# Tables of gates and overflow built from 16-bit one-hots that the routing keeps, and the first expert's weights split by other engines in another order

## The chip, the cores and the metric

The program runs on one core of a Trainium2 chip, as one launch. The metric is the device time of one execution in microseconds, the median over several runs. The core has a matrix engine (TensorE, PE in the profile; its weight loads are the track PEld), a vector engine (VectorE, DVE), an activation engine (ScalarE, ACT), GpSimd (POOL) and a queue engine (SyncE, SP) that issues the loads of the weights. Every engine works through its own list of instructions in order; semaphores order them against each other.

## The reference

Two layers. The first mixes tokens by a gated MLP and a gated convolution, the second by sliding-window attention; each is followed by a norm, a mixture of 32 experts (two for each token) and another norm. The change touches the mixture of experts only:

```
g_idx = argmax(x @ w_grp); e_sel = (x @ w_exp)[group g_idx]
top_p, top_i = top_k(softmax(e_sel), 2);  gates = g_p * top_p / sum(top_p)
# rows sorted by expert, in blocks of 128 rows: row_tok, row_gate, blk_e
def run_block(xb, e): return (silu(xb @ wg[e]) * (xb @ wu[e])) @ wd[e]
out = segment_sum(ys * row_gate, row_tok)
```

There are 1024 tokens with 1024 channels; an expert has 512 hidden channels, all in 32-bit floats.

## The kernel before

**Weights.** All weights come in chunks of 1 MB (tiles `raw` and `ry`, 128x2048). For the products each is split in two: ScalarE writes the high part (`h`, line 164), and VectorE subtracts it from the chunk for the low part (`l`, line 165). A 32-bit product is then three TensorE products, h by xh, l by xh and h by xl (lines 204 to 206, `mm3`). `split_until(i)` writes both parts of all chunks up to the i-th; `pump` then issues the next load into the room that came free. An expert has six chunks: two of `w_gate`, two of `w_up`, two of `w_down`. The h and l tiles of chunks lie in two places of two buffers each, so four chunks can be split at a time.

**Routing** (`proj_route`). For each of eight blocks n of 128 tokens: output projection (`pm`), residual and norm (`norm`, on `xr`, with a power on GpSimd at line 258 between the two halves), transposes (`transp`), the router's products (`logits`, into `pl`), the choice of the first and the second expert (`choose`, `choose2`, line 470 and around), a product that counts earlier tokens with the same expert (`rank`), the slot of each token (`place`, which makes a one-hot row `oh` for it), and the table of tokens by expert and slot (`tabulate`, into `pidx`). The steps of the blocks overlap. After the last block's projection the tail is left: `norm`, `transp`, `logits`, `choose`, `choose2`, `rank`, `place` and `tabulate` of block 7, with those of block 6 between them, and the first three chunks of the first expert, whose low parts GpSimd makes there (`eng=nc.gpsimd`). `warm(n)` are products for nothing, on TensorE, between the steps. The tail ends with `idx` (line 598), the table of tokens.

**Experts** (`experts`). `gather(e)` fetches an expert's rows by an indirect transfer that GpSimd issues (line 703). `xpose` transposes them into `pt`, `xsplit` splits them into `xh` and `xl`, `gu` makes the products with gate and up weights (`pg`, `pu`), `hid_pose` transposes and splits the hidden rows, `down` makes the last products and `y_out` adds the rows, times their gates (`sgate`), to the result. The order is written out by hand. Between the products `extra(e)` takes the next piece of a generator: the gates, then the table of gates by slot (`slot_gates`, 16 products into `pgate`, from one-hots `goh` and rows `ga` that GpSimd makes), then the bookkeeping of rows beyond an expert's 128 (`overflow`, 16 products into `pov`, from `ooh` and `orr` that VectorE makes). There are three such places in an expert, each behind `split_until`.

The first expert's split rows lie in the room of the results:

```
th, tl = ("xh", "xl") if e > 0 else ("yt0", "yt1")
h = w.tile([P, 8, P], F32R, name=f"xh{e}", tag=th, bufs=1)
lo = w.tile([P, 8, P], F32R, name=f"xl{e}", tag=tl, bufs=1)
```

A tag with `bufs=1` has one room: a new tile in it waits until all that reads the tile before it is done.

Of the kernel before, what the change touches and what calls it, by code (L numbers as in the profile page):

```python
# [19 lines left out]
P = 128  # L20
# [5 lines left out]
NG = 4  # L26
# [9 lines left out]
def moe_net_kernel(ctx, tc, a, dbg=None):  # L36
# [76 lines left out]
    st = {"load": 0, "split": 0, "hlb": None, "rawb": None, "xT": None,  # L113
# [3 lines left out]
    def pump(eng=nc.sync):  # L117
        while st["load"] < min(len(chunks), st["limit"]):
# [13 lines left out]
            if i == 1:  # L132
                # the first two chunks come in alternate quarters, that the work may start
# [12 lines left out]
    # 32 KB in two halves: the mixers' output, chunks, the norm's rows, heads of q  # L146
# [19 lines left out]

    def split_until(i, eng=None, high=None):
        while st["split"] <= min(i, len(chunks) - 1):
            j = st["split"]
            st["split"] += 1  # L170
            where = chunks[j][1]
            if where in ("a", "b"):
                p = hla if where == "a" else st["hlb"]
                h = p.tile([P, 2048], F32R, name=f"h{j}", tag="h" + where, bufs=2)
                l = p.tile([P, 2048], F32R, name=f"l{j}", tag="l" + where, bufs=2)
            else:
                k = 2 * where[1]
                h = st["xT"][0][:, k:k + 2, :].rearrange("p k f -> p (k f)")
                l = st["xT"][1][:, k:k + 2, :].rearrange("p k f -> p (k f)")
            hs[j], ls[j] = h, l  # L180
# [7 lines left out]
            elif j in (mark["qkv"] - 1, len(chunks) - 1):  # L188
                for o in (0, 1024):
                    split_to(*(c[:, o:o + 1024] for c in (h, l, x)), eng)  # L190
            else:
                split_to(h, l, x, eng, high)
# [3 lines left out]
    def warm(n, ps, tag, bufs):  # L196
        # products for nothing where the tensor engine waits, that its clock stays up
# [12 lines left out]
    # -------------------------------------------------------------- constants  # L210
# [54 lines left out]
    # ------------------------------------------------- bias rows of attention  # L265
# [3 lines left out]
    def bias_rows(w, ps):  # L269
# [11 lines left out]
        # row q lies q further right, so that a plain rectangle of it holds the relative positions  # L281
# [25 lines left out]
            # v, tokens on partitions  # L307
# [26 lines left out]
            # u, channels on partitions  # L334
# [15 lines left out]
            # spatial mixing of v and y_a  # L350
# [12 lines left out]
            # gated convolution  # L363
# [261 lines left out]
    def slot_gates(w, ps, R):  # L625
        pt = ps.tile([P, 512], F32, name="pgate", tag="misc", bufs=1)
        made, used = [], 0
        for make, use in ((4, 0), (2, 0), (4, 4), (6, 6), (0, 0), (0, 6)):
# [10 lines left out]
            if used < 16:  # L639
                yield  # L640
# [810 lines left out]
```

## Time and profile before

| what | value |
|---|---|
| time, median of 3 runs | 2085.58 us (2083.27 to 2086.29) |
| profiled execution, its time from first to last instruction (span) | 2086.2 us |
| TensorE busy | 1931.8 us, 93% |
| VectorE busy | 1580.8 us, 76% |
| ScalarE busy | 1206.1 us, 58% |
| GpSimd busy | 476.9 us, 23% |
| mean rate of the transfers | 253 GB/s |
| mean granted clock of TensorE | 0.962 of full |

The profiled execution has no other time listed than its span; it lies within 0.03% of the median. Busy times are shares of the whole program, whose stages differ; the stages are read apart by their place in time. The routing's tail lies at 340 to 372 us in the first layer and at 1367 to 1399 us in the second, the experts behind each.

### The profile page before, as it was taken

The page shows a single profiled execution, that of the slowest core. Times are in us where ns is not written, and L with a number is a line of the kernel's source. Part 1 is how long each engine was busy: PE and PEld are TensorE (multiplying, and loading weights), DVE is VectorE, ACT ScalarE, POOL GpSimd, SP SyncE. Part 2 cuts the span into 40 slices and gives each one's busy share as a digit, 9 for nine tenths or more (in the row PEclk, how much of TensorE's full clock was granted, in tenths as well). Part 3 has the DMA queues.
Part 4 walks back from the last instruction along what each step waited for, and adds up shares of the span by engine and source line. Part 5 has one row for each costly group of instructions (what it writes and reads, how often), then busy time and mean ns, then how long its engine had stood idle before and what let it go on. Part 6 is the DMA issues. An engine that isn't in the chain of part 4 may idle for free. (4 is left out here: it accounts for less than half of the span.)

```text
span 2086.2 us, 24852 instructions
## 1 busy us (share of the span) xinstructions
PE 1931.8 (93%) x9264; PEld 1565.7 (75%) x9264; DVE 1580.8 (76%) x2020; ACT 1206.1 (58%) x1246; POOL 476.9 (23%) x319
## 2 busy tenths in 40 slices
PE   8999998899999999998598989979999999999990
PEld 7888786687778888887487767757877888888870
DVE  3533587599888888887643996976898888888876
ACT  4211211477677777776454872125777777777763
POOL 0100003622111211212300552146121112112116
PEclk9999998899999999999799999989999999999995
DMA  6141536599969999997511006366999699999983
GB/s 249 41 122 41 192 112 242 192 335 371 345 228 363 371 364 377 369 371 281 225 41 62 21 21 232 125 248 219 374 357 355 218 379 360 368 376 364 380 282 145
DMA packets 97215, 527.59 MB, mean 253 GB/s; under 512 B 19668, under 2 KB 21732, under 8 KB 43840
## 3 DMA queue, kind: packets, MB, share of 16 engines
q1 hardware_dynamic: 76992, 487.41, 61.6%
q0 software_dynamic: 20096, 38.52, 7.4%
q8 instruction: 75, 1.23, 0.2%
q14 instruction: 52, 0.43, 0.1%
HBM read 501.58 MB, written 62.94 MB: 271 GB/s over the span
## 5 line engine op out<-in xcount | busy, mean ns | idle before, releaser
L165 DVE TENSOR_TENSOR l<-raw,h 128x2048 fp32r<-128x2048 f32 (+2 forms) x356 | 797.4, 2261 | 108.3 <-ACT h L164 104.0
L164 ACT CAST h<-raw 128x2048 fp32r<-128x2048 f32 (+1 forms) x363 | 678.2, 1884 | 130.9 <-PE pu L206 38.0
L713 POOL DMA_INDIRECT acc<-y,idx x64 | 127.5, 1993 | 605.7 <-ACT y L764 578.9
L204 PE MATMUL pu<-h,xh 128*128 128x512 f32 x512 | 209.5, 409 | 0.0
L204 PE MATMUL pg<-h,xh 128*128 128x512 f32 x512 | 208.6, 407 | 0.0
L204 PE MATMUL pd<-h,hh 128*128 128x512 f32 x512 | 203.2, 397 | 1.4 <-ACT hh L164 1.4
L206 PE MATMUL pg<-h,xl 128*128 128x512 f32 x512 | 203.0, 397 | 1.0 <-DVE xl L165 1.0
L206 PE MATMUL pu<-h,xl 128*128 128x512 f32 x512 | 203.1, 397 | 0.0
L205 PE MATMUL pu<-l,xh 128*128 128x512 f32 x512 | 202.9, 396 | 0.0
L206 PE MATMUL pd<-h,hl 128*128 128x512 f32 x512 | 202.0, 395 | 0.0
L205 PE MATMUL pg<-l,xh 128*128 128x512 f32 x512 | 201.7, 394 | 0.0
L205 PE MATMUL pd<-l,hh 128*128 128x512 f32 x512 | 201.4, 393 | 0.0
L703 POOL DMA_INDIRECT xg<-x1d,idx x64 | 96.6, 1510 | 354.0 <-PE pt L735 340.2
L164 ACT CAST xh<-pt 128x1024 fp32r<-128x1024 f32 x66 | 67.0, 1016 | 126.5 <-PE pu L205 110.2
L848 DVE TENSOR_TENSOR sg<-sg,pu 128x512 f32<-128x512 f32 x64 | 44.0, 687 | 110.8 <-PE pu L206 110.8
L206 PEld LDWEIGHTS pg<-h,xl 128*128 128x128 f32 x512 | 96.0, 188 | 25.2 <-DVE xl L165 1.9
L206 PEld LDWEIGHTS pd<-h,hl 128*128 128x128 f32 x512 | 96.0, 187 | 24.9 <-DVE hl L165 0.9
L206 PEld LDWEIGHTS pu<-h,xl 128*128 128x128 f32 x512 | 96.6, 189 | 23.7
L165 DVE TENSOR_TENSOR l<-ry,h 128x2048 fp32r<-128x2048 f32 x48 | 109.9, 2296 | 5.9 <-ACT h L164 5.9
L204 PEld LDWEIGHTS pd<-h,hh 128*128 128x128 f32 x512 | 96.0, 187 | 24.4 <-ACT hh L164 1.7
L205 PEld LDWEIGHTS pd<-l,hh 128*128 128x128 f32 x512 | 96.0, 187 | 23.1
L204 PEld LDWEIGHTS pu<-h,xh 128*128 128x128 f32 x512 | 97.6, 191 | 20.1
(326 smaller groups left out, 3844.8 us busy)
## 6 DMA issues: line engine op xcount, KB each, us to landing
raw<-in_w_gate SPq DMA_DIRECT2D x128, 1024.0 KB, 8.3
raw<-in_w_up SPq DMA_DIRECT2D x104, 1024.0 KB, 10.5
raw<-in_w_down SPq DMA_DIRECT2D x104, 1024.0 KB, 10.6
ry<-in_w_up SPq DMA_DIRECT2D x24, 1024.0 KB, 8.1
ry<-in_w_down SPq DMA_DIRECT2D x24, 1024.0 KB, 10.0
raw<-in_w_in SPq DMA_DIRECT2D x8, 1024.0 KB, 6.4
x1d<-xr SPq DMA_DIRECT2D x16, 512.0 KB, 2.7
acc<-xr SPq DMA_DIRECT2D x16, 512.0 KB, 3.9
```

Source lines behind the costliest of these rows:

```text
L164: (high or nc.scalar.copy)(h, x)
L165: (eng or nc.vector).tensor_tensor(l, x, h.bitcast(F32), op=OP.subtract)
L204: nc.tensor.matmul(out, sh, mh, start=start, stop=False)
L205: nc.tensor.matmul(out, sh, ml, start=False, stop=False)
L206: nc.tensor.matmul(out, sl, mh, start=False, stop=stop)
L703: nc.gpsimd.indirect_dma_start(out=rows, out_offset=None, in_=src, in_offset=bass.IndirectOffsetOnAxis(ap=idx, axis=0), bounds_check=T - 1 ...
L713: nc.gpsimd.indirect_dma_start(out=acc, out_offset=bass.IndirectOffsetOnAxis(ap=idx, axis=0), in_=rows, in_offset=None, bounds_check=T - 1 ...
L848: nc.vector.tensor_tensor(sg, sg, pu, op=OP.mult)
```

## The change

Four things are changed, in both layers.

1. **The tail of the routing.** GpSimd makes no low parts there. ScalarE writes the high parts of all four chunks ahead of the last norm (`highs(c0 + 7)`); VectorE makes the first low part behind that norm, the second and third behind the first gather, the fourth behind the first expert's rows. `choose2` and `rank` of block 6 stand ahead of the norm of block 7 and of the 15 products for nothing.
2. **The first gather.** The second gather and VectorE's first work on the gates stand behind a tiny `memset` on GpSimd, which stands behind the first gather.
3. **The table of gates.** The routing's one-hots are kept as 16-bit floats (`R["oh"]`). A gate is cut into three 16-bit parts (`gate_parts`); VectorE multiplies them with the experts' one-hots into `ag` (in the room `yt1`), and 16 products with 16-bit operands and 96 columns stand together where before a part of 32-bit ones stood. `add_parts` sums the three parts.
4. **The overflow table.** Likewise: nine VectorE instructions that each do for all or for a quarter of the 16 groups, one in each extra, then 16 products of 64 columns together.

```diff
-                oh = w.tile([P, 2, P], F16, name=f"oh{n}", tag="oh", bufs=2)
+                oh = R["oh"][:, 2 * n:2 * n + 2]
...
-            warm(15, ps, "pm", 3)
             st["free"]["rawx"] = 2
             pump()
-            split_until(c0 + 4, eng=nc.gpsimd)
+            choose2(NB - 2)
+            rank(NB - 2)
+            warm(15, ps, "pm", 3)
+            highs(c0 + 7)
             norm(NB - 1)
-            choose2(NB - 2)
-            split_until(c0 + 5, eng=nc.gpsimd)
             transp(NB - 1)
+            split_until(c0 + 4)
+            place(NB - 2)
             warm(4, ps, "pm", 3)
-            rank(NB - 2)
-            place(NB - 2)
-            split_until(c0 + 6, eng=nc.gpsimd)
             logits(NB - 1)
...
-        ge = w.tile([P, NB, NG], F32, name="ge")
+        ge = w.tile([P, NB * NG], F32, name="ge", tag="inc", bufs=2).rearrange("p (n g) -> p n g", n=NB)
+        nc.gpsimd.memset(ge[:, 0, 0:1], 0.0)
+        yield
...
     def slot_gates(w, ps, R):
+        gate_parts(w, R)
+        yield
+        A = R["A"].rearrange("p n j e -> p (n j) e")
+        ag = w.tile([P, 16, 3, NE], F16, name="ag", tag="yt1", bufs=1)
+        for c in range(3):
+            nc.vector.tensor_tensor(ag[:, :, c], A, R["gp"][:, c, :, None].to_broadcast([P, 16, NE]), op=OP.mult)
+            if c > 0:
+                yield
         pt = ps.tile([P, 512], F32, name="pgate", tag="misc", bufs=1)
-        made, used = [], 0
-        for make, use in ((4, 0), (2, 0), (4, 4), (6, 6), (0, 0), (0, 6)):
...
-                nc.gpsimd.tensor_scalar(oh, slots, R["pos"][:, n, j:j + 1], None, op0=OP.is_equal)
-                nc.gpsimd.tensor_scalar(ag, R["A"][:, n, j], R["gate"][:, n, j:j + 1], None, op0=OP.mult)
...
+        for i in range(16):
+            nc.tensor.matmul(pt[:, 0:3 * NE], R["oh"][:, i], ag[:, i].rearrange("p c e -> p (c e)"),
+                             start=(i == 0), stop=(i == 15))
+        add_parts(R["sgate"], [pt[:, c * NE:(c + 1) * NE] for c in range(3)])
+        yield
...
             gather(0)
-            gather(1)
             gen = gates(w, R)
             next(gen)
-            split_until(c0 + 3)
+            gather(1)
+            next(gen)
+            split_until(c0 + 2)
             xpose(0)
             xsplit(0)
+            split_until(c0 + 3)
```

GpSimd's list around the tail of the first layer's routing, before: `l_2471`, `l_2499` and `l_2533` are low parts of the first expert's first three chunks, `mvn` is the norm's power, `xg` the gathered rows.

```order
L258 TENSOR_TENSOR mvn_2330<-mvn_2330,half 128x1
L165 TENSOR_TENSOR l_2471<-raw_1326,h_2470 128x2048
L258 TENSOR_TENSOR mvn_2478<-mvn_2478,half 128x1
L165 TENSOR_TENSOR l_2499<-raw_1497,h_2498 128x2048
L165 TENSOR_TENSOR l_2533<-raw_1503,h_2532 128x2048
L703 DMA xg_1460<-x1d_1442,idx_1452 128x1024
L703 DMA xg_1461<-x1d_1442,idx_1452 128x1024
L703 DMA xg_1460<-x1d_1442,idx_1452 128x1024
L636 TENSOR_SCALAR goh_2697<-slots,pos_1450 128x128
```

The same place in the changed kernel (its line 272 is line 258 of before, 748 is 703):

```order
L272 TENSOR_TENSOR mvn_2326<-mvn_2326,half 128x1
L272 TENSOR_TENSOR mvn_2492<-mvn_2492,half 128x1
L748 DMA xg_1461<-x1d_1442,idx_1452 128x1024
L620 MEMSET ge 128x1
L748 DMA xg_1462<-x1d_1442,idx_1452 128x1024
L748 DMA xg_1461<-x1d_1442,idx_1452 128x1024
```

The three low parts are gone from GpSimd, and the memset stands between the first two gathers.

VectorE's list in the first expert, before, from the gates' end (`gate`) to the low part of that expert's seventh chunk in order (`l_2809`); `xl_2789` is the low part of the second expert's rows, `sg` the product of its two halves:

```order
L623 TENSOR_TENSOR gate_1451<-pr,gs 128x16 [waits DVE_49]
L165 TENSOR_TENSOR l_2726<-raw_1511,h_2725 128x2048 [waits Activation_49]
L165 TENSOR_TENSOR l_2754<-raw_1513,h_2753 128x2048 [waits PE_49,Activation_49]
L165 TENSOR_TENSOR xl_2789<-pt_2779,xh_2788 128x1024 [waits Activation_49]
L848 TENSOR_TENSOR sg_2739<-sg_2739,pu_2672 128x512 [waits PE_49]
L165 TENSOR_TENSOR l_2809<-ry_2235,h_2808 128x2048 [waits DMAHW4_49,Activation_49]
```

The same place in the changed kernel, behind the gate's parts (`gp`), where `ag` is the new table and `xl_2749` and `sg_2718` are those tiles; the wait of the first `ag` is for TensorE's last product into `pu_2666`, the last that reads the room `yt1`:

```order
L651 TENSOR_SCALAR gp<-gr 128x16 [waits DVE_49]
L165 TENSOR_TENSOR l_2710<-raw_1512,h_2709 128x2048 [waits Activation_49]
L667 TENSOR_TENSOR ag<-A_1447,gp 128x16x32 [waits PE_49]
L667 TENSOR_TENSOR ag<-A_1447,gp 128x16x32
L165 TENSOR_TENSOR l_2733<-raw_1514,h_2732 128x2048 [waits Activation_49]
L667 TENSOR_TENSOR ag<-A_1447,gp 128x16x32 [waits DVE_49]
L165 TENSOR_TENSOR xl_2749<-pt_2739,xh_2748 128x1024 [waits Activation_49]
L895 TENSOR_TENSOR sg_2718<-sg_2718,pu_2666 128x512
L165 TENSOR_TENSOR l_2769<-ry_2232,h_2768 128x2048 [waits Activation_49]
```

Three `ag` instructions stand ahead of `xl_2749` now, the first of them with a wait for TensorE, and a low part between them.

## Rows read from the trace of the kernel before

**Rows 1.** Stages: start, end, length; busy PE, PEld, DVE, ACT, POOL; clock; DMA; GB/s.
```profile
357.00:365.00 8.00, 7.68 (x34) 5.57 (x33) 3.98 (x20) 2.81 (x2) 3.02 (x1) 0.50 0.72 263
...
640.00:700.00 60.00, 60.00 (x280) 49.33 (x279) 50.81 (x29) 46.01 (x33) 12.45 (x7) 1.00 0.99 359
```

**Rows 2.** Timeline of the first layer's routing tail (start, duration, engine, line, instruction).
```profile
340.12 1.95 PE L463 MATMUL pl<-rw,xt 128*128 128x36 f32 x16
...
342.23 4.62 POOL L165 TENSOR_TENSOR l<-raw,h 128x2048 fp32r<-128x2048 f32 x1 [7.07 <-ACT h L164]
...
342.53 4.33 DVE L470 SCALAR_TENSOR_TENSOR t<-lg,mx,wt 128x4 f32<-128x4 f32 x1
...
345.90 0.39 PE L206 MATMUL pm<-h,yx 128*128 128x512 f32 x1
...
346.19 3.40 PE L200 MATMUL warm<-ones 128*128 128x512 f16 x15
...
348.46 0.68 DVE L437 SCALAR_TENSOR_TENSOR xr<-xr,pm 128x512 f32<-128x512 f32 x1
...
351.40 4.97 DVE L263 SCALAR_TENSOR_TENSOR xr<-xr,mvn,l1b 128x512 f32<-128x512 f32 x1 [0.44 <-POOL mvn L258]
...
357.07 0.75 DVE L263 SCALAR_TENSOR_TENSOR xr<-xr,mvn,l1b 128x512 f32<-128x512 f32 x1
...
360.60 3.61 PE L463 MATMUL pl<-rw,xt 128*128 128x36 f32 x16
...
364.67 1.83 DVE L470 SCALAR_TENSOR_TENSOR t<-lg,mx,wt 128x4 f32<-128x4 f32 x1
...
371.73 0.19 DVE L598 TENSOR_SCALAR idx<-pidx 128x32 int32<-128x32 f32 x1 [0.27 <-PE pidx L529]
```

**Rows 3.** Line 470 over the whole program: duration in ns, min/median/max.
```profile
L470 DVE SCALAR_TENSOR_TENSOR t<-lg,mx,wt x16: 221/223/4340, 258.2 to 1391.5; 128x4 f32<-128x4 f32 x16
```

**Rows 4.** Timeline of the first expert's start and of its last product's reader.
```profile
372.48 0.17 DVE L608 TENSOR_TENSOR ee<-mx 128x8 f32<-128x8 f32 x1
...
372.80 1.15 POOL L703 DMA_INDIRECT xg<-x1d,idx  x1 [6.32 <-DVE ee L608]
...
378.55 1.01 ACT L164 CAST xh<-pt 128x1024 fp32r<-128x1024 f32 x1 [2.56 <-PE pt L735]
...
378.79 0.99 POOL L703 DMA_INDIRECT xg<-x1d,idx  x1 [3.52 <-PE pt L735]
...
393.71 0.69 DVE L848 TENSOR_TENSOR sg<-sg,pu 128x512 f32<-128x512 f32 x1 [0.51 <-PE pu L206]
```

**Rows 5.** Timeline of TensorE around the table of gates, second expert (idle before, releaser).
```profile
396.77 1.42 PE L630 MATMUL pgate<-ga,goh 128*128 128x32 f32 x12
...
403.72 0.30 PE L630 MATMUL pgate<-ga,goh 128*128 128x32 f32 x2
406.65 0.64 PE L630 MATMUL pgate<-ga,goh 128*128 128x32 f32 x2 [2.63 <-POOL ga L637]
...
410.79 1.95 PE L735 MATMUL pt<-ident,xg 128*128 128x128 f32 x8
```

**Rows 6.** TensorE's waits, second layer's experts: total us, times, longest.
```profile
PE pov L698 <- DVE orr L696: 4.2, 5, 1.9
...
PEld pov L698 <- DVE orr L696: 6.4, 5, 2.3
```

**Rows 7.** Timeline of TensorE, two products of the overflow table that waited.
```profile
520.96 0.41 PE L698 MATMUL pov<-orr,ooh 128*128 128x32 f32 x2 [1.90 <-DVE orr L696]
...
542.18 0.41 PE L698 MATMUL pov<-orr,ooh 128*128 128x32 f32 x2 [0.58 <-DVE orr L696]
```

**Rows 8.** VectorE's instructions by group, 372 to 600 us: busy us, mean ns.
```profile
L165 DVE TENSOR_TENSOR l<-raw,h 128x2048 fp32r<-128x2048 f32 x43 | 97.8, 2284 | 9.9 <-ACT h L164 9.9
...
L165 DVE TENSOR_TENSOR xl<-pt,xh 128x1024 fp32r<-128x1024 f32 x12 | 14.6, 1218 | 1.8 <-ACT xh L164 1.8
...
L676 DVE TENSOR_TENSOR cmp<-A,ovs 128x512 f32<-128x512 f32 x1 | 0.7, 683 | 0.0
```

More of the change, by code (lines that the diff above doesn't have):

```diff
@@ L165, in split_to, with highs, target @@
         (eng or nc.vector).tensor_tensor(l, x, h.bitcast(F32), op=OP.subtract)
+    def highs(i):
+        for j in range(st["split"], i + 1):
+            target(j)
+            nc.scalar.copy(hs[j], raws[j])
+            st["highs"] = j
+    def target(j):
+        where = chunks[j][1]
+        if where in ("a", "b"):
+            p = hla if where == "a" else st["hlb"]
+            h = p.tile([P, 2048], F32R, name=f"h{j}", tag="h" + where, bufs=2)
+            l = p.tile([P, 2048], F32R, name=f"l{j}", tag="l" + where, bufs=2)
+        else:
+            k = 2 * where[1]
+            h = st["xT"][0][:, k:k + 2, :].rearrange("p k f -> p (k f)")
+            l = st["xT"][1][:, k:k + 2, :].rearrange("p k f -> p (k f)")
+        hs[j], ls[j] = h, l
     def split_until(i, eng=None, high=None):
@@ L170, in split_until @@
             st["split"] += 1
[L171 to L180, printed above, removed]
+            if j > st["highs"]:
+                target(j)
+            h, l = hs[j], ls[j]
             x = raws.pop(j)
@@ L623, in gates @@
         nc.vector.tensor_tensor(R["gate"], pr, s[:, :, 3:4].to_broadcast([P, NB, 2]), op=OP.mult)
-    def slot_gates(w, ps, R):
-        pt = ps.tile([P, 512], F32, name="pgate", tag="misc", bufs=1)
-        made, used = [], 0
-        for make, use in ((4, 0), (2, 0), (4, 4), (6, 6), (0, 0), (0, 6)):
-            for i in range(used, used + use):
-                nc.tensor.matmul(pt[:, 0:NE], *made[i], start=(i == 0), stop=(i == 15))
-            used += use
-            for i in range(len(made), len(made) + make):
-                n, j = i // 2, i % 2
-                oh = w.tile([P, P], F32, name=f"goh{i}", tag="goh", bufs=6)
-                ag = w.tile([P, NE], F32, name=f"ga{i}", tag="ga", bufs=6)
-                nc.gpsimd.tensor_scalar(oh, slots, R["pos"][:, n, j:j + 1], None, op0=OP.is_equal)
-                nc.gpsimd.tensor_scalar(ag, R["A"][:, n, j], R["gate"][:, n, j:j + 1], None, op0=OP.mult)
-                made.append((oh, ag))
-            if used < 16:
-                yield
-        nc.vector.tensor_copy(R["sgate"], pt[:, 0:NE])
+    PARTS = (1.0, 2.0 ** -11, 2.0 ** -22)
@@ new lines, in gate_parts, with add_parts @@
+    def gate_parts(w, R):
+        gp = R["gp"] = w.tile([P, 3, 16], F16, name="gp")
+        rest = w.tile([P, 16], F32, name="gr")
+        x = R["gate"].rearrange("p n j -> p (n j)")
+        for c in range(3):
+            nc.vector.tensor_scalar(gp[:, c], x, 1.0 / PARTS[c], None, op0=OP.mult)
+            if c < 2:
+                nc.vector.scalar_tensor_tensor(rest, gp[:, c], -PARTS[c], x, op0=OP.mult, op1=OP.add)
+                x = rest
+    def add_parts(out, parts):
+        nc.vector.tensor_copy(out, parts[0])
+        for c in (1, 2):
+            nc.vector.scalar_tensor_tensor(out, parts[c], PARTS[c], out, op0=OP.mult, op1=OP.add)
@@ L688, in overflow @@
         nc.vector.scalar_tensor_tensor(slot, q, -float(P), pos, op0=OP.mult, op1=OP.add)
+        rr = w.tile([P, 16, 4, 16], F16, name="orr", tag="cmp", bufs=1)
+        sel = rr[:, :, 0]
+        nc.vector.tensor_tensor(sel, slots[:, None, 0:16].to_broadcast([P, 16, 16]),
+                                oid[:, :, None].to_broadcast([P, 16, 16]), op=OP.is_equal)
+        yield
+        for c in range(3):
+            nc.vector.tensor_tensor(rr[:, :, c + 1], sel, R["gp"][:, c, :, None].to_broadcast([P, 16, 16]), op=OP.mult)
+            yield
+        sel = sel.rearrange("p (n j) b -> p n j b", j=2)
+        nc.vector.tensor_tensor(sel, sel, rowm[:, :, None, None].to_broadcast([P, NB, 2, 16]), op=OP.mult)
+        yield
+        for i in range(0, 16, 4):
+            nc.vector.tensor_tensor(R["oh"][:, i:i + 4], slots[:, None, :].to_broadcast([P, 4, P]),
+                                    slot[:, i:i + 4, None].to_broadcast([P, 4, P]), op=OP.is_equal)
+            yield
         po = ps.tile([P, 512], F32, name="pov", tag="misc", bufs=1)
-        gate = R["gate"].rearrange("p n j -> p (n j)")
         for i in range(16):
-            oh = w.tile([P, P], F32, name=f"ooh{i}", tag="goh", bufs=6)
-            rr = w.tile([P, 2, 16], F32, name=f"orr{i}", tag="ga", bufs=6)
-            nc.vector.tensor_scalar(oh, slots, slot[:, i:i + 1], None, op0=OP.is_equal)
-            for j, x in enumerate((rowm[:, i // 2:i // 2 + 1], gate[:, i:i + 1])):
-                nc.vector.tensor_scalar(rr[:, j], slots[:, 0:16], oid[:, i:i + 1], x, op0=OP.is_equal, op1=OP.mult)
-            yield
-            nc.tensor.matmul(po[:, 0:32], oh, rr.rearrange("p j b -> p (j b)"), start=(i == 0), stop=(i == 15))
+            nc.tensor.matmul(po[:, 0:64], R["oh"][:, i], rr[:, i].rearrange("p c b -> p (c b)"),
+                             start=(i == 0), stop=(i == 15))
+        yield
         nc.vector.tensor_scalar(R["ovidx"], po[:, 0:16], float(T), None, op0=OP.add)
-        nc.vector.tensor_copy(R["ovgate"], po[:, 16:32])
+        add_parts(R["ovgate"], [po[:, 16 + 16 * c:32 + 16 * c] for c in range(3)])
     def gather_rows(rows, src, idx):
```

12 lines of the change are left out of this document (8 added, 4 removed).

## The prediction

> **What bounds the kernel now.** The chain that ended last follows only the final store and says nothing of the experts, so I started from the table of stages. In the steady part of the first layer's experts TensorE is busy for all of 60 us at full clock, and the transfers run at 0.99 of their share beside it [rows 1]: TensorE sets the pace there, with the loads close behind. What the change touches lies elsewhere: in the routing's tail, where TensorE waits for VectorE, and at two tables that TensorE waits for in the experts. The timeline of the tail shows what is late. VectorE's line 470, of 0.22 us as a rule [rows 3], takes 4.33 us; it began 0.3 us behind a subtraction on GpSimd of 4.62 us and ended with it, at 346.86 [rows 2]. Line 263 takes 4.97 us where its neighbour takes 0.75, and line 470 takes 1.83 us once more [rows 2]. VectorE stands still while GpSimd makes low parts. The second layer repeats it: the longest case of line 470, 4.34 us, is there [rows 3].
>
> **The routing's tail, part by part**, in us for one layer. The end is `idx`, at 371.73 to 371.92.
>
> *Up to the norm.* The last product into `pm` ends at 346.29, but the norm's first instruction, line 437, starts at 348.46 [rows 2], behind the delayed line 470 and 1.6 us of the same choice. Without the delay of 4.1 the choice is done at 344.4. `choose2` of block 6, now moved ahead of the norm, is about as long as that rest (an estimate: 1.6) and ends at 346.0, before TensorE does. `rank` waits for it no longer than for its own place on TensorE. With 0.2 for a semaphore the norm starts at 346.5: 2.0 gained.
>
> *In the norm.* Line 263 falls from 4.97 to 0.75: 4.2 gained.
>
> *From the norm to the logits.* The rows are done at 357.82, the logits at 364.21 [rows 2]. Before, TensorE had nothing between the end of the 15 products, at 349.6, and that of the norm's first half, at 356.4 [rows 2]; its clock is 0.50 throughout 357 to 365 [rows 1], and the eight logits take 3.61 where block 6's took 1.95 at full clock [rows 2]. Now that half is there at about 350.2, just behind the products for nothing, so I expect full clock: 1.7 gained, and 0.4 as the four products and `rank` that stood ahead of the logits were slow too. 2.1 in all. VectorE's new work here, the first low part (2.28 [rows 8]) and `place` (about 1.2, an estimate), takes 3.5 of the 4.0 until the logits are there: hidden. Without that cover it would cost 3.5. ScalarE's four high parts wait for the projection's chunks to be read, the last until 346.3, and none of them stands near the copy of the transposes, some 6 us later.
>
> *The choice.* The second delayed line 470 falls from 1.83 to 0.22: 1.6 gained. The products for nothing must leave room for `rank`: 16 at the pace of 15 in 3.40 [rows 2] end together with the choice.
>
> *The first gather.* It starts at 372.80, 0.9 behind `idx` and 0.15 behind the last of VectorE's three gate instructions; a later gather started 0.3 after the transposes that it waited for, with VectorE idle [rows 4]. Now VectorE is kept away by the memset: 0.6 gained. The bounds are 0 and 0.7. [...]
>
> *Behind the gather.* VectorE then has the gates (0.6) and two low parts (2 x 2.28) before `xl` of the first expert. Gather (0.3 + 1.15), memset (0.1, an estimate; at most the 1.0 of a gather) and these end 7.0 after `idx`; the rows' high part, 7.6 after it before [rows 4], is then there at 7.0. I take 0.3 lost; with a memset of 1.0, or if the second gather holds VectorE as the low parts did, it is 1.5. The fourth low part fits behind.
>
> Sum: 2.0 + 4.2 + 2.1 + 1.6 + 0.6 - 0.3 = **10.2**.
>
> **The table of gates.** Before, its 16 products come in groups of 4, 6 and 6. Six take some 1.3 [rows 5], four 0.8. The last group goes from 403.72 to 410.79, 7.1, as GpSimd makes its rows too late, and at half clock the next transposes and products lose about 1.1 more (eight transposes in 1.95 [rows 5]). In all 10.3, which go. What comes: 16 products of 16 bits, whose price no row has. One of 512 columns takes 3.40 / 15 = 0.23 [rows 2], so 96 columns cost between 0.04 and 0.23: 0.7 to 3.6, and I take 1.2, nearer the small end since the columns are a fifth.
>
> And a new wait comes. `ag` lies in the room `yt1`, which holds the low part of the first expert's rows until the last product into `pu`. The first `ag` therefore waits for TensorE to finish the first expert's gate and up products, which end just before 393.71 in the run before [rows 4]. Behind it in VectorE's list stand the second `ag`, a low part, the third `ag` and `xl` of the second expert; TensorE's third product for that expert needs this `xl`. So TensorE stands for 3 x 0.68 + 2.28 + 1.22 = 5.5 (`ag` has 512 elements in a row like the 0.683 one [rows 8]). Before, `xl` was made while TensorE worked. [...] Net gain 10.3 - 1.2 - 5.5 - 1.9 = **1.7**, with bounds of -2 and 4.
>
> **The overflow table.** TensorE's five waits for `orr` are 4.2 from the products' modelled ends and 6.4 from its weight loads [rows 6]; I take 5.0. The 16 products themselves are some 0.14 to 0.24 each [rows 7], 2.8. The 16 new ones, of 64 columns, cost between 0.5 and 3.6, taken as 1.0. They stand at the middle extra of an expert, where four products waited 0.6 for what the extra before had made [rows 7]; the last quarter of the one-hots is made there too, so one such wait stays: 0.6. Its VectorE work falls from three instructions in each of 16 extras to one in each of 9. Gain 5.0 + 2.8 - 1.0 - 0.6 = **6.2**, with bounds of 4 and 8.
>
> **Sum.** 10.2 + 1.7 + 6.2 = 18.1 for a layer, 36.2 for two. Against the profile's own span of 2086.2 that is 2050.0; the median lies 0.6 below that span, which gives **2049.5**. Since TensorE is full behind these places, an earlier start moves everything behind it; twelve chunks are loaded ahead in the first twelve experts, so the loads follow.
>
> **The rivals.**
> - *The table of gates does not hold VectorE up* (A): the room is free in time, or `xl` is not missed. Then 5.5 + 1.9 come back for each layer: 2034.7. For it, only that other waits in the experts hide. Against it, the order of the list. Chance 0.08.
> - *TensorE stays at half clock in the tail* (B): it was at 0.50 there [rows 1]. The logits lose 1.7 and the 16 products take 7.3, so `rank` comes about 2.9 late more: 4.6 for a layer, 2058.7. Against it: the gaps fall below 1 us. Chance 0.10.
> - *The loads bound the experts* (C): at 0.99 of their share [rows 1] they give TensorE nothing more, and 7.9 for a layer is lost: 2065.3. Against it: what TensorE waited for in these stretches was VectorE's tables [rows 6]. Chance 0.10, a third of it with the routing's gain lost too, which is no change.
> - *VectorE never held the first gather up* (R): the 0.9 from `idx` to its start is its own, and 0.6 less is gained for a layer, 2050.7. For it: `idx` is the last that it needs, and the row names VectorE only as what ended last. Against it: the 0.3 of the later gather [rows 4]. Chance 0.09. [...]
> - *Slower* (D): the new stop of 5.5 leaves TensorE at half clock, in the second expert, for long. Half a microsecond is lost for each at half clock, so from 40 us of it in a layer (2 x (18.1 + 1.9)) nothing is gained, and beyond it the kernel is slower. With 50 us at half clock 25 are lost where 1.9 are counted: 25 - 1.9 - 18.1 = 5 slower in each layer, 2095.6. Against it: after 410.79 the loss was small, as TensorE's work was dense again. Chance 0.03.
>
> **How the numbers follow.** The forecast itself has 0.60. The bounds of its terms all together would give 2040 to 2064; as they will not fall on one side, its own range is 2042 to 2057. The range of 2033 to 2061 holds it with R, most of B and half of A, about 0.8. A change of less than 0.2%, 4.2 us, can hardly be told from none; faster by more than that has 0.94, within it 0.03 (a third of C), slower 0.03 (D).
>
> **What the profile of the changed kernel would show.** Lines 470 and 263 (their new numbers) with no case much above 0.3 and 0.8 us; the logits of block 7 in about 2 us; granted clock 1.00 through the tail; `idx` some 10 us earlier; the first gather 0.3 behind `idx`. In the waits of TensorE, GpSimd's `ga` gone, `pov` once at under 1 us, and a new one of about 5 us, twice, for VectorE's `xl` at the second expert. Wrong would be: a clock of 0.50 before the first gather (B), waits of ScalarE for `raw` in the experts (C), or no wait for `xl` (A).

## The result, and the profile after

The changed kernel takes 2039.87 us (median of 4 runs, 2037.52 to 2042.99), the kernel before 2085.77 in the same runs: 45.9 us less, a ratio of 0.9778 (0.9764 to 0.9792). The forecast was 2049.5 us, 36.2 less: the measured time lies within the stated 2033 to 2061, and below the forecast's own range of 2042 to 2057. The profiled execution spans 2037.1 us, 49.1 below that of before; the sums below are made against these two spans. They differ by 3.2 more than the medians: the changed kernel's profiled execution, 2038.65 us by its time, was 1.2 below its median, and the rest lies with that of before, whose time is not listed. Line numbers moved: 470 is now 484, 263 is 277, 463 is 477, 703 is 748, 735 is 780.

The stages of the changed kernel (columns as in [rows 1]):

```profile
340.00:360.00 20.00, 17.93 (x106) 11.54 (x105) 16.76 (x62) 10.08 (x7) 0.92 (x1) 1.00 0.68 252
360.00:380.00 20.00, 16.47 (x79) 11.55 (x80) 14.43 (x31) 7.72 (x8) 4.13 (x5) 1.00 0.62 214
380.00:400.00 20.00, 15.14 (x70) 11.92 (x69) 13.11 (x13) 9.09 (x8) 0.76 (x1) 0.83 0.49 174
...
640.00:700.00 60.00, 60.00 (x278) 49.59 (x277) 52.71 (x31) 47.48 (x33) 10.83 (x6) 1.00 1.01 379
```

The clock is 1.00 through the tail, where it was 0.50 from 357 to 365 [rows 1]; up to the end of this layer's experts it falls only at 380 to 400. The transfers use 1.01 of their share in the steady part, before 0.99.

The tail's timeline, first layer, for [rows 2] and the start of [rows 4]:

```profile
346.79 0.69 DVE L451 SCALAR_TENSOR_TENSOR xr<-xr,pm 128x512 f32<-128x512 f32 x1 [0.20 <-PE pm L220]
...
349.74 0.75 DVE L277 SCALAR_TENSOR_TENSOR xr<-xr,mvn,l1b 128x512 f32<-128x512 f32 x1 [0.44 <-POOL mvn L272]
...
351.19 0.75 DVE L277 SCALAR_TENSOR_TENSOR xr<-xr,mvn,l1b 128x512 f32<-128x512 f32 x1
...
353.80 1.98 PE L477 MATMUL pl<-rw,xt 128*128 128x36 f32 x16 [0.29 <-ACT xt L471]
...
361.41 0.19 DVE L613 TENSOR_SCALAR idx<-pidx 128x32 int32<-128x32 f32 x1 [0.27 <-PE pidx L543]
...
362.47 1.15 POOL L748 DMA_INDIRECT xg<-x1d,idx  x1 [12.77 <-DVE idx L613]
...
366.84 1.20 PE L780 MATMUL pt<-ident,xg 128*128 128x128 f32 x8 [2.01 <-DMA xg<-x1d,idx]
```

Both instructions of line 277 take 0.75, the logits 1.98, and `idx` comes 10.3 earlier. No case of the choice's first instruction is held any more (duration in ns, min/median/max over the program; for [rows 3]):

```profile
L484 DVE SCALAR_TENSOR_TENSOR t<-lg,mx,wt x16: 222/223/226, 258.6 to 1356.2; 128x4 f32<-128x4 f32 x16
```

TensorE's waits in the first layer from 340 us on (total, times, longest; for [rows 6]):

```profile
PE pg L220 <- DVE xl L165: 5.4, 2, 4.9
...
PE pov L741 <- DVE oh L736: 0.6, 1, 0.6
```

GpSimd's `ga` is gone, the overflow table waits once, and the new wait for `xl` is there, in the second layer with the same 5.4. The timeline around it (second expert, VectorE and TensorE):

```profile
382.31 1.29 DVE L667 TENSOR_TENSOR ag<-A,gp 128x512 f16<-128x512 f32 x2 [4.66 <-PE pu L220]
382.33 0.40 PE L219 MATMUL pg<-l,xh 128*128 128x512 f32 x1
...
383.52 2.29 DVE L165 TENSOR_TENSOR l<-raw,h 128x2048 fp32r<-128x2048 f32 x1
385.72 0.69 DVE L667 TENSOR_TENSOR ag<-A,gp 128x512 f16<-128x512 f32 x1
386.32 1.22 DVE L165 TENSOR_TENSOR xl<-pt,xh 128x1024 fp32r<-128x1024 f32 x1
...
387.59 0.79 PE L220 MATMUL pg<-h,xl 128*128 128x512 f32 x1 [4.86 <-DVE xl L165]
388.19 0.63 PE L218 MATMUL pg<-h,xh 128*128 128x512 f32 x1
...
392.87 1.21 PE L672 MATMUL pgate<-ag,oh 128*128 128x96 f16 x16
393.90 0.48 PE L218 MATMUL pg<-h,xh 128*128 128x512 f32 x1
```

VectorE waits 4.66 for the first expert's last product into `pu`, then makes the five things in the order of its list (two `ag`, a low part, the third `ag`, `xl`) while TensorE stands for 4.86. The products behind it are 0.63 long in place of 0.39, at about half clock (0.53 from 387 to 394), until the table's products.

Where the 49.1 us come from is read at one mark that both kernels share, the start of the transposes of an expert's rows (`pt`; 0 is the first expert, 32 the overflow's block), in us:

| expert | layer 1 before | after | gained | layer 2 before | after | gained |
|---|---|---|---|---|---|---|
| 0 | 377.31 | 366.84 | 10.47 | 1404.32 | 1366.92 | 37.40 |
| 3 | 430.35 | 417.78 | 12.57 | 1457.51 | 1417.90 | 39.61 |
| 7 | 503.24 | 490.23 | 13.01 | 1530.41 | 1490.35 | 40.06 |
| 13 | 623.15 | 600.19 | 22.96 | 1648.78 | 1600.31 | 48.47 |
| 31 | 951.17 | 926.23 | 24.94 | 1976.80 | 1926.48 | 50.32 |
| 32 | 982.25 | 957.13 | 25.12 | 2007.89 | 1960.56 | 47.33 |

The last product into `pm` ahead of the tail starts 0.46 later than before in layer 1 (346.36 to 345.90) and 26.32 earlier in layer 2 (1346.36 to 1372.68). So the tail gave 10.9 and 11.1. The table of gates lies between 0 and 3, the overflow table between 7 and 13. Between 13 and 31 nothing was changed, and still 0.11 is gained with every expert: its period, from one expert's transposes to the next one's, is 18.11 in place of 18.22.

### The profile page after: what moved, and what is told of

Its sections match the earlier page's. It is cut to its first block, busy times and chain, and to the rows that moved or that the text cites. A ratio compares the mean times of both kernels' runs of the same rounds, so it can differ in the third digit from the quotient of the medians.

```text
span 2037.1 us, 24598 instructions
## 1 busy us (share of the span) xinstructions
PE 1898.8 (93%) x9200; PEld 1548.7 (76%) x9200; DVE 1567.2 (77%) x1972; ACT 1206.1 (59%) x1246; POOL 408.7 (20%) x251
## 5 line engine op out<-in xcount | busy, mean ns | idle before, releaser
L164 ACT CAST h<-raw 128x2048 fp32r<-128x2048 f32 (+2 forms) x355 | 663.4, 1884 | 131.1 <-PE pu L220 23.7
L220 PE MATMUL pg<-h,xl 128*128 128x512 f32 x512 | 204.8, 400 | 10.7 <-DVE xl L165 10.7
L748 POOL DMA_INDIRECT xg<-x1d,idx x64 | 108.4, 1693 | 398.2 <-PE pt L780 366.7
L165 DVE TENSOR_TENSOR l<-ry,h 128x2048 fp32r<-128x2048 f32 x48 | 109.3, 2287 | 7.0 <-ACT h L164 7.0
L218 PEld LDWEIGHTS pg<-h,xh 128*128 128x128 f32 x512 | 97.9, 191 | 20.4 <-issue 0.6
L219 PEld LDWEIGHTS pg<-l,xh 128*128 128x128 f32 x512 | 97.4, 190 | 20.5
```

What stands on the lines that cost most here:

```text
L164: (high or nc.scalar.copy)(h, x)
L165: (eng or nc.vector).tensor_tensor(l, x, h.bitcast(F32), op=OP.subtract)
L218: nc.tensor.matmul(out, sh, mh, start=start, stop=False)
L219: nc.tensor.matmul(out, sh, ml, start=False, stop=False)
L220: nc.tensor.matmul(out, sl, mh, start=False, stop=stop)
L748: nc.gpsimd.indirect_dma_start(out=rows, out_offset=None, in_=src, in_offset=bass.IndirectOffsetOnAxis(ap=idx, axis=0), bounds_check=T - 1 ...
```

## The experiments

**The room of `ag`.** The first expert's low part goes to two rooms that are empty until the hidden rows:

```diff
-                th, tl = ("xh", "xl") if e > 0 else ("yt0", "yt1")
...
+                else:
+                    los = [w.tile([P, 4, P], F32R, name=f"xl0{i}", tag=t, bufs=1) for i, t in enumerate(("hh", "hlo"))]
+                    nc.scalar.copy(h, xT[e])
+                    for i in range(2):
+                        k = slice(4 * i, 4 * i + 4)
+                        nc.vector.tensor_tensor(los[i], xT[e][:, k], h[:, k].bitcast(F32), op=OP.subtract)
```

> The changed kernel, but the low part of the first expert's rows lies in the rooms of the later hidden parts (tags hh and hlo), so that the products ag find their room yt1 empty. Theory: the new stop of TensorE (4.86 us idle, then about 2.5 us lost at half clock, in each layer) was caused by that room alone. Then VectorE makes ag during the first expert, no wait of TensorE for xl at the second expert stays, its clock stays 1.00 there, and the time falls by 2 x 7.4 = 15 us, to about 2025. Rival 1: xl is late for another reason (the order of VectorE's list): the wait stays above 3 us and the time at about 2040. Rival 2: the loads take the gain back at the ends of the layers, where TensorE already waits for the last chunk: 2030 to 2037, with longer waits of ScalarE for raw.

Measured: 2025.45 us (2022.87 to 2030.63), ratio to before 0.9711 (0.9695 to 0.9727), 14.4 below the changed kernel (16.1, when each is set against the kernel before of its own runs). TensorE at the same place:

```profile
383.54 0.50 PE L220 MATMUL pg<-h,xl 128*128 128x512 f32 x1 [0.70 <-DVE xl L165]
...
386.42 0.84 PE L672 MATMUL pgate<-ag,oh 128*128 128x96 f16 x16
```

The stop is 0.70, the clock 1.00 from 380 to 400, and at expert 31 of the second layer this kernel is 14.2 ahead of the changed one. The room alone made the stop, at 7 us a layer. The table's 16 products take 0.66 here, at full clock (386.42 to the next product at 387.08).

**The tail alone.** The kernel before with the new tail (all edits of `proj_route`, `highs`, and the start of `experts`), but the old tables:

```diff
-            split_until(c0 + 4, eng=nc.gpsimd)
+            choose2(NB - 2)
+            rank(NB - 2)
+            warm(15, ps, "pm", 3)
+            highs(c0 + 7)
             norm(NB - 1)
...
+        nc.gpsimd.memset(ge[:, 0, 0:1], 0.0)
+        yield
```

> The kernel before, with only the routing's tail changed (high parts ahead of the norm, low parts on VectorE, the choice and rank of block 6 ahead of it, the memset that holds VectorE until the first gather is issued); the tables of gates and overflow are the old ones. Theory: the tail is worth 10.9 us in the first layer and some 11 in the second, as the two traces show at idx, and the tables are worth the rest: 2085.8 - 22 = about 2064, the steady period of an expert still 18.22 us. Rival: the tail's gain is partly the tables' (one-hots kept, less work on GpSimd later) or is eaten by the table of gates, which GpSimd now begins at another time: 2070 to 2080.

Measured: 2070.48 us, ratio 0.9919 (0.9903 to 0.9936): 17.0 less, not 22. At the first expert's transposes 10.7 are gained, at expert 4 only 7.9. GpSimd and TensorE between:

```profile
381.08 0.41 PE L647 MATMUL pgate<-ga,goh 128*128 128x32 f32 x2 [2.10 <-POOL ga L654]
...
391.27 4.40 POOL L654 TENSOR_SCALAR ga<-A,gate 128x32 f32<-128x32 f32 x1
395.65 2.56 POOL L653 TENSOR_SCALAR goh<-slots,pos 128x128 f32<-128x128 f32 x1
...
398.60 0.41 PE L647 MATMUL pgate<-ga,goh 128*128 128x32 f32 x2 [2.47 <-POOL ga L654]
```

A `ga` of 0.36 us takes 4.40 beside low parts on VectorE, and TensorE waits for the table twice for over 2 us, 5.9 in all; in the kernel before once, 3.8 in all. The old table of gates takes some 3 us of the tail's gain in each layer. That is the rival, not the theory.

**The tables alone.** The reverse: the changed kernel with the old tail, GpSimd's low parts and the old start of the experts:

```diff
-            highs(c0 + 7)
+            split_until(c0 + 4, eng=nc.gpsimd)
             norm(NB - 1)
...
-        nc.gpsimd.memset(ge[:, 0, 0:1], 0.0)
-        yield
```

> The kernel before with only the tables of gates and overflow changed (16-bit products from the kept one-hots, gate parts, the shared rooms); the routing's tail and the start of the experts are the old ones, GpSimd's low parts among them. The tail alone gave 17 us (2070.5), as the old table of gates lost 3 us more in each layer once the tail was new, GpSimd making its rows beside VectorE's low parts. Theory: the two parts help each other, so the tables alone give 2 x (2.0 gates + 8.5 overflow + 3.3 shorter period) = 27.6, less 0 to 3 at the end for the loads: about 2059. Rival: the parts add up, and the tables alone give 2085.8 - (2070.5 - 2039.9) = 2055; or most of the period's share is lost to the loads, as in the run with 32 unused bytes: 2064.

Measured: 2062.33 us, ratio 0.9882 (0.9859 to 0.9906), 24.5 less. At expert 31 of the second layer the tables alone have gained 27.1, the tail alone 18.1, both together 50.3. By the traces, one execution of each, the two help each other by 5.1 us; by the medians it is 4.4 (45.9 - 24.5 - 17.0), which the noise of the three could make alone. What speaks for it is the place where the tail alone loses its 3 us in each layer: the new table leaves GpSimd nothing to make where the new tail puts work on VectorE.

**Without the hold.** The `memset` and its place in the order are taken out:

```diff
-        nc.gpsimd.memset(ge[:, 0, 0:1], 0.0)
-        yield
...
             gather(0)
+            gather(1)
             gen = gates(w, R)
             next(gen)
-            gather(1)
-            next(gen)
             split_until(c0 + 2)
```

> The changed kernel without the memset that holds VectorE until the first gather is issued: VectorE's three instructions of the gates follow idx at once, as in the kernel before, and both gathers stand behind each other on GpSimd. Theory (the rival of the prediction that VectorE never held the gather up): the gather starts 0.87 us behind the end of idx here too, and nothing is lost, 2038 to 2041; the first expert's low parts may even start some 2 us earlier on VectorE. Rival (the step of the prediction): the gather starts 0.6 us later, behind the last of VectorE's three instructions, and 1.2 us go in all, about 2041; and if the low parts that follow hold the second gather up for 4.5 us, nothing of it is seen, as it is needed 10 us later.

Measured: 2047.54 us, ratio 0.9812 (0.9789 to 0.9834): 7.7 more than the changed kernel (6.7, when each is set against the kernel before of its own runs), which neither expected. The timeline:

```profile
361.60 0.19 DVE L613 TENSOR_SCALAR idx<-pidx 128x32 int32<-128x32 f32 x1 [0.27 <-PE pidx L543]
...
362.43 4.49 DVE L204 TENSOR_TENSOR l<-raw,h 128x2048 fp32r<-128x2048 f32 x2
362.66 3.07 POOL L746 DMA_INDIRECT xg<-x1d,idx  x1 [12.78 <-DVE ee L624]
366.04 1.78 POOL L746 DMA_INDIRECT xg<-x1d,idx  x1 [0.31 <-issue]
...
370.82 1.53 PE L778 MATMUL pt<-ident,xg 128*128 128x128 f32 x6 [5.80 <-DMA xg<-x1d,idx]
```

The gather starts 0.87 behind the end of `idx` here too. But a low part began 0.23 ahead of it; the gather takes 3.07 in place of 1.15, and TensorE gets the rows 8.2 after its start, in place of 4.4. From the end of `idx` to the first transposes it is 3.8 more than in the changed kernel in the first layer and 4.0 in the second. The longer gather is 1.9 of this; why the rows come another 1.9 later was not followed up.

**One operand in place of two.** The same kernel, with two reductions on VectorE over a weight tile that is there already ahead of the low parts:

```diff
+            for i in range(2):
+                nc.vector.tensor_reduce(R["ovgate"][:, i:i + 1], hs[c0].bitcast(F32), axis=AX.X, op=OP.max)
             split_until(c0 + 2)
```

> The kernel without the hold, and in front of its two low parts two reductions on VectorE over a weight tile of 128x2048 that is there already, about 2.2 us each, whose results nothing needs: instructions with one operand, while the first gather is issued. [...] Then the gather takes 1.15 us here, in place of 3.07 without the hold, and its rows are there for TensorE 4.4 us after the gather's start, in place of 8.1. Rival: any long VectorE instruction holds the gather: it takes 3 us or more, its rows come 8 us after its start. The time itself lies some 4 us a layer above that of the changed kernel either way, as the low parts come later.

Measured: 2048.77 us in one run, before 2093.67 beside it, which says little of the time. The timeline:

```profile
362.08 4.47 DVE L853 TENSOR_REDUCE ovgate<-h 128x1 f32<-128x2048 f32 x2
362.32 1.15 POOL L746 DMA_INDIRECT xg<-x1d,idx  x1 [12.78 <-DVE ee L624]
...
366.47 4.48 DVE L204 TENSOR_TENSOR l<-raw,h 128x2048 fp32r<-128x2048 f32 x2
366.87 1.20 PE L778 MATMUL pt<-ident,xg 128*128 128x128 f32 x8 [2.19 <-DMA xg<-x1d,idx]
...
368.34 3.48 POOL L746 DMA_INDIRECT xg<-x1d,idx  x1 [3.54 <-PE pt L778]
```

Beside instructions of the same length with one operand the gather takes 1.15 and its rows are there 4.55 after its start. The third gather, issued beside the low parts, takes 3.48. But a low part differs from these reductions in two things: it has a second operand in SBUF, the memory of the tiles, and it writes 2048 columns where they write one. The trace of the kernel before with 32 unused bytes (below) has a case that tells them apart, a gather issued 0.29 into a subtraction of VectorE with one operand in SBUF and the other in PSUM, the memory of TensorE's sums, which writes 512 columns:

```profile
2026.33 0.69 DVE L165 TENSOR_TENSOR hl<-ph,hh 128x512 fp32r<-128x512 f32 x1 [1.45 <-ACT hh L164]
2026.62 1.05 POOL L703 DMA_INDIRECT xg<-acc,ovidx  x1 [10.96 <-DMA acc<-y,idx]
```

With 0.40 of it left the gather takes 1.05; with 0.38 to 0.48 of a low part left, gathers took 1.25 or more. So in these traces it is the second operand from SBUF that holds a gather up, though against the writing there is this one clear case. The low parts do it everywhere: of 606 gathers in the eleven traces that were issued with more than 0.15 of a low part left, 596 ended 0.85 to 1.10 behind that low part. In the changed kernel TensorE waits for gathered rows at the first expert of a layer alone (2.0 and 2.1 us), so only there a held gather costs something.

**Products of the overflow table later.** The kernel before, each product two extras behind the making of its rows:

```diff
-            yield
-            nc.tensor.matmul(po[:, 0:32], oh, rr.rearrange("p j b -> p (j b)"), start=(i == 0), stop=(i == 15))
+            made.append((oh, rr))
+            yield
+            for k in range(i - 1, i if i < 15 else i + 1):
+                if k >= 0:
+                    oh, rr = made[k]
+                    nc.tensor.matmul(po[:, 0:32], oh, rr.rearrange("p j b -> p (j b)"), start=(k == 0), stop=(k == 15))
```

> The kernel before, with each product of the overflow table two extras behind the making of its rows, where it stood one behind; products and VectorE's work stay as they are. Theory: the five waits for orr in a layer cost 6.3 us from start to start of TensorE's products (2.3 once and 1.0 four times), more than the 4.2 that the products' ends show, and in the first layer 1.4 more at half clock; without them 12 to 14 us go in all, and experts 9 to 12 fall from 19.7 us to 18.7. Time about 2073. Rival 1: VectorE is the bound of that stage, so that the wait comes back elsewhere, for xl or the low parts l: 2080 to 2086. Rival 2: the waits are worth what the products' ends show, 2 x 4.2: 2077.

Measured: 2075.07 us, ratio 0.9940 (0.9920 to 0.9960): 11.7 less. No wait of TensorE is left from 500 to 640 us. From expert 7 to 13 it takes 112.87 in both layers, where before took 119.91 and 118.37: the waits cost 7.0 and 5.5. At full clock that is less than the theory's 6.3, which takes the distance of two starts as a whole; 0.23 of it a product takes anyway. The difference of the layers is the clock: in the second layer of before it is 1.00 throughout. In the first layer, first the window of before, then that of this kernel:

```profile
520.00:530.00 10.00, 9.04 (x38) 7.55 (x39) 6.75 (x13) 3.88 (x3) 1.05 (x1) 0.83 1.02 361
```

```profile
520.00:530.00 10.00, 10.00 (x50) 8.32 (x49) 10.00 (x14) 7.14 (x6) 1.85 (x2) 1.00 1.01 344
```

What is left above six plain experts (6 x 18.22 = 109.3) is 3.55 for the 16 old products.

**32 unused bytes.** The kernel before with one more tile in front of the experts' own:

```diff
             w = pool(f"mw{l}", st=s)
+            w.tile([P, 8], F32, name=f"pad{l}")
```

> The kernel before, with nothing but 32 unused bytes in each partition put ahead of the experts' tiles, so that the rows' high and low parts xh, xl, hh, hlo start at a multiple of 64 bytes, as they do in the changed kernel by chance (before: 32 beyond one). Theory: the steady period of an expert, 18.22 us before and 18.12 after, follows from where these tiles lie; half the products then follow each other in 0.229 us in place of 0.233, and some 7 us go: about 2079. Rival: the period follows from the work that the change takes from VectorE and GpSimd, or from the loads: period 18.22, time 2085.8, within 0.2%.

Measured: 2085.16 us, ratio 0.9987 (0.9977 to 0.9997). The transposes of two neighbouring experts in before, in the changed kernel and with the 32 bytes:

```profile
823.60 1.11 PE L735 MATMUL pt<-ident,xg 128*128 128x128 f32 x8
...
841.83 1.11 PE L735 MATMUL pt<-ident,xg 128*128 128x128 f32 x8
```

```profile
799.45 1.11 PE L780 MATMUL pt<-ident,xg 128*128 128x128 f32 x8
...
817.55 1.11 PE L780 MATMUL pt<-ident,xg 128*128 128x128 f32 x8
```

```profile
821.16 1.11 PE L736 MATMUL pt<-ident,xg 128*128 128x128 f32 x8
...
839.26 0.99 PE L736 MATMUL pt<-ident,xg 128*128 128x128 f32 x7
```

The period is the changed kernel's, 18.10 to 18.12, so the place of the tiles makes it, and not the work. But of the 7 us only 2.3 are seen in the time. In its trace 1.6 go in the second layer, between experts 7 and 8 (22.53 in place of 20.97), 1.5 at its last two steps, and 0.8 by a later start, in one execution; about 1 us more was not found.

**All weights at multiples of 64 bytes**, in the changed kernel:

```diff
-        gp = R["gp"] = w.tile([P, 3, 16], F16, name="gp")
-        rest = w.tile([P, 16], F32, name="gr")
+        gp = R["gp"] = w.tile([P, 4, 16], F16, name="gp")
+        rest = w.tile([P, 16], F32, name="gr", tag="slot", bufs=1)
...
+            "pad": p.tile([P, 8], F32, name=f"pad{l}"),
```

> The changed kernel, with tiles shifted by 32 bytes so that the second pair of weight rings, the gathered rows and the split projection input too start at multiples of 64 bytes (a 32-byte unused tile, one table widened by 32 bytes, one small tile in another's room). Theory: the products that read the weights of that ring follow each other in 0.234 us and those of the other in 0.229; with both at 0.229 an expert takes 0.2 us less, 13 us in all, if the loads can follow: 2027. Rival 1: the transfers, at 0.99 of their share, cannot follow, and TensorE waits for them near the ends: 2033 to 2040. Rival 2: the placement has nothing to do with it: 2039.9, period 18.12.

Measured: 2039.85 us, ratio to before 0.9770 (0.9752 to 0.9788), as the changed kernel. The period fell again, to 18.00 here and 18.05 for the next expert, 18.03 in the mean, by 0.08 and not by 0.2:

```profile
798.97 1.11 PE L780 MATMUL pt<-ident,xg 128*128 128x128 f32 x8
...
816.97 1.12 PE L780 MATMUL pt<-ident,xg 128*128 128x128 f32 x8
```

The reason in the theory does not hold either. With both places of the weights' tiles (the rings of the theory) at multiples of 64 bytes the products do not all follow each other at 0.229: 24 products into `pd` start from 802.70 to 807.92, those of the next expert from 820.68 to 826.04, 0.227 and 0.233 apart. From the first expert to the overflow's block 1.9 are gained on the changed kernel in the first layer and 3.7 in the second; 0.7 had been lost up to the first expert, 3.0 go between the layers and 2.7 behind the last block. Whether the loads take the gain back (rival 1) is thus not shown.

**Room and shifts together.**

> The room for ag of the first experiment (2025.45) and the 32-byte shifts of the fourth (2039.85, steady period 18.03 in place of 18.11) together. Theory: the shorter period is there again, and as in the run with the shifts alone the loads take it back at the end of each layer's experts: 2020 to 2026, with ScalarE waiting for raw in the last third of the second layer's experts. Rival: with 15 us won at the start of each layer the loads keep their lead, and 64 x 0.08 = 5 us remain: 2020 or less.

Measured: 2025.71 us, ratio 0.9700 (0.9677 to 0.9723): the room alone had 2025.45. At the end of the first layer's experts it is 3.4 ahead of the room alone, and 4.1 at the first product into `pm` of the second layer's projection (1222.55 and 1226.66). By the logits of that projection's second block it is 2.2 behind (1263.43 and 1261.27), so 6.3 are lost there, and 3.4 more at the last expert (34.31 to the overflow's block, where the room alone takes 30.88). For the first loss, the window 1235 to 1260, the room alone and then both:

```profile
1235.00:1260.00 25.00, 23.96 (x121) 19.60 (x120) 17.93 (x37) 3.33 (x6) 9.19 (x5) 1.00 0.76 316
```

```profile
1235.00:1260.00 25.00, 22.40 (x89) 18.27 (x88) 15.53 (x31) 2.45 (x4) 6.60 (x4) 0.80 0.62 259
```

Part of it is TensorE at half clock, 0.80 in the mean. Whether that goes with the shifts or is chance of one execution was not settled.

## Why the prediction was right, and where it was wrong

The three gains that were forecast came where the prediction had them, and each at least as large. What carries the time below the forecast's own range is a gain that the prediction knew nothing of, 6.9 us from a shorter period; a loss at the last expert takes 3.0 of it back. Without both the time would be some 2044, inside that range. (The forecast's last step, 2050.0 less 0.6, is 2049.4 and not 2049.5.)

**The tail** was right in its steps but one. Measured in the first layer: the norm starts 1.67 earlier though TensorE came 0.46 later, 2.1 (2.0 in the prediction, whose 0.2 for a semaphore was an estimate: in the changed kernel the norm starts 0.04 behind the modelled end of that last product, 346.36 + 0.39); in the norm 4.2 (4.2); from the norm's rows to the logits 6.39 before and 3.84 after, 2.5 (2.1), at full clock; from the logits to `idx` 7.52 and 5.63, 1.9 (1.6). What ScalarE and VectorE took over stayed hidden.

**The step that failed is the first gather**: "Now VectorE is kept away by the memset: 0.6 gained." Nothing was gained. In the first layer the gather starts 0.87 or 0.88 behind the end of `idx` in the five kernels read for it (before, changed, tail alone, without the hold, with reductions), in the second 0.83, whatever VectorE does, so these 0.87 are its own, and the later gather's 0.3 was no measure for it. On the start, rival R was right. For the hold itself the prediction named the wrong thing: it does not bring the gather forward, it keeps the low parts, which the change puts behind it, from standing in its way, and that is worth the 7.7 us (or 6.7) of the run without it. Beside low parts gathers took 3.07 and 3.48, beside reductions 1.15; what in a gather waits for a low part, no run here shows.

**Behind the gather** nothing was lost: from the end of `idx` to the first product it is 7.59 in the first layer, before 7.74 (0.3 lost in the prediction, whose terms for VectorE here add up to 6.7 and not to the 7.0 that it states). The memset took 0.12 (0.1, an estimate).

**The table of gates** was right: 1.7 forecast for a layer; the table shows 2.10 and 2.21, of which 0.33 are the shorter period. The stop is 4.86 (5.5), half clock costs 2.4: ten products 0.43 apart in place of 0.23, and the transposes of the hidden rows, at a clock of 0.53 from 387 to 394. The 1.9 that the forecast's sum takes for it was the author's estimate, which no run shows. The 16 products take 1.03, partly at half clock, and 0.66 at full clock (1.2). That the room holds `ag` up, and that its price was some 7 us with the clock, the first experiment shows: 14.4 us for both layers. Rival A is thus not what this kernel does, but what it could do.

**The overflow table** was mis-sized, 6.2 for a layer against 9.3 and 7.8 (9.95 and 8.41 in the table, less six shorter periods). The five waits cost 7.0 and 5.5, not 5.0. At full clock, in the second layer, that is between the two readings of [rows 6], 4.2 and 6.4. The starts of products tell it best: at a wait that shows as 0.58 they lie 0.98 apart (541.20 and 542.18 in the kernel before) in place of 0.23, so it costs 0.75; the long one costs 2.07 (518.66 to 520.96), and one long and four short ones 5.1. What the prediction left out is the 1.5 more in the first layer, where TensorE went on at half clock behind the long wait (0.51 from 522.6 to 526). The old products cost 3.55, not 2.8, and all of the new 1.3, not 1.6.

**What the sum did not have** is the shorter period: 6.9 us over both layers, from where the experts' tiles came to lie when the old rooms were dropped. The experiment with 32 bytes shows that this is no merit of the new tables, though in the time of that run only 2.3 of it are left. Against it the last expert of the second layer takes 3.0 longer than before, since the last weights are late:

```profile
PE pd L218 <- ACT hh L164: 1.5, 1, 1.5
...
PE pd L220 <- DVE hl L165: 0.8, 1, 0.8
```

These are TensorE's waits of the changed kernel, 1340 to 1965 us; before, the first was 0.7. From 1955 to 1961 the clock is 0.72. ScalarE, which makes `hh`, starts on the last two pieces of `w_down` at 1952.47, 0.4 ahead of TensorE's transposes of the hidden rows; before it was 3.3 ahead (2000.10 and 2003.42). Its instruction in the changed kernel and in the kernel before:

```profile
1952.47 2.00 ACT L164 CAST h<-raw 128x1024 fp32r<-128x1024 f32 x2 [2.77 <-DMA raw<-in_w_down]
```

```profile
2000.10 2.00 ACT L164 CAST h<-raw 128x1024 fp32r<-128x1024 f32 x2 [2.77 <-DMA raw<-in_w_down]
```

That is rival C in small: the loads are close behind everywhere, as [rows 1] said, and TensorE meets them at the end. The sign that the prediction named for C did come: in the second layer's experts ScalarE waits for `raw` 20 times, 25.3 us in all, before 15 times and 14.6. It costs TensorE nothing until the last expert.

Added up against the spans, forecast 36.2, and beyond it: tail +1.6, gates +0.2, overflow +4.6, period +6.9, last expert -3.0, a late start of the first tail -0.5, and 1.2 gained between the layers and 1.8 behind the last expert, neither followed up, and both no more than executions of one kernel differ by: 49.0 of 49.1. Rivals B and D did not come: the clock was 1.00 in the tail, and about half behind the new stop (0.53 from 387 to 394, in the second layer 0.57 from 1386 to 1394), and beside that only 0.72 at the last expert.

## What to carry to other kernels

Before reusing a room for something new, look who reads the old tile last: here a table of 2 us of work, put into the wrong 4 KB, cost 7 us in each layer, and two other rooms that were empty gave it back. A gather through GpSimd that others wait for is worth issuing ahead of a long VectorE subtraction of two SBUF tiles, by a dependency: here, 0.23 us behind the start of one, it took 3.07 in place of 1.15, and its rows came 3.8 us later. A part of a gain can come from where tiles happen to lie (here a period of 18.11 in place of 18.22): a kernel with a few unused bytes tells that apart in one run. And a new tail that puts work on VectorE lost 3 us a layer to the old table, whose rows GpSimd made beside it: try the parts of a change alone before adding up what they gave.

## What the runs showed of the hardware that was not expected

- An indirect gather issued 0.23 us after the start of a VectorE subtraction of two SBUF tiles took 3.07 us and its rows came 8.2 after its start; beside reductions of the same length, with one operand, 1.15 and 4.55. Beside a subtraction with one operand in PSUM one took 1.05. Of 606 gathers issued while such a subtraction of two SBUF tiles had more than 0.15 left, 596 ended 0.85 to 1.10 behind its end.
- Moving the experts' tiles by 32 bytes, those of the rows from 32 beyond a multiple of 64 bytes to a multiple, took the period of an expert (72 products of 512 columns) from 18.22 to 18.11. The products followed each other at 0.233 us before; after, at 0.229 with weights in the place that starts at a multiple of 64 bytes too and at 0.234 with those in the place that starts 32 beyond. This gives no rule: with all at multiples they follow each other at 0.227 to 0.233 (period 18.03), and in the first experiment's kernel, whose hidden rows start 32 beyond, the products into `pd` take 0.229 with weights that start 32 beyond and 0.234 with the others. Why is open.
- A wait of TensorE that shows as 0.58 us put the starts of two products 0.98 apart in place of 0.23.
